# Down's operand 128 bytes lower in SBUF, and 56 instead of 48 products between a norm's sums and the transposes of its factors

## The chip, the cores and the metric

One core of one Trainium2 chip runs the whole program. The metric is device time in microseconds (us) of one execution, from the hardware profiler; lower is better.

## What is computed

A small transformer on one sequence of 256 tokens with 1024 channels, in float32. Two layers, each made of an FFN, a mixer, a second FFN and a per-layer embedding (ple), and behind them one hybrid layer with an FFN of its own and a last norm. Cut to what the change touches:

```python
def rms_norm(x, g):
    return x * rsqrt(mean(x * x, -1) + EPS) * g

def swiglu(h, w_gate, w_up, w_down):          # 1024 -> 2816 -> 1024
    return (silu(h @ w_gate) * (h @ w_up)) @ w_down

for i in range(2):
    x = x + 0.5 * swiglu(rms_norm(x, g[0]), ...)               # FFN i-0
    x = x + (even_mixer if i == 0 else mla_mixer)(rms_norm(x, g[1]), ...)
    x = x + 0.5 * swiglu(rms_norm(x, g[2]), ...)               # FFN i-1
    x = x + ple(rms_norm(x, g[3]), p[i], ...)
x = x + concat(moba, ssd, pool)(rms_norm(x)) @ w_out            # hybrid
x = x + swiglu(rms_norm(x), ...)                                # the last FFN
```

## The kernel before

Activations lie transposed, channels on the 128 partitions and the 256 tokens along a row, as eight tiles `self.x`. TensorE's float32 is replaced by products of numbers rounded to a short mantissa (fp32r): each operand is split into a high part and the rest, and each weight tile of 128x128 takes three products, high by high, rest by high, high by rest. One product is a weight load of 128x128 and a matmul with 256 columns moving; `mm` (line 163) issues them all. The moving operand of the gate and up projections are the rows `hh`/`hl` (`self.hT`, eight pairs of tiles in the pool `cp`); that of the Down projection are pieces of tiles named `big` (list `aT`, pool `sp`), which also serve elsewhere as work space. All weights stream from memory in pieces of 1 MB (`load_piece`), queued on SP; ACT rounds each half to `whi` (line 259) and DVE forms `wlo` (line 260).

`ffn` calls `fm` for gate and up, 44 column blocks in 22 groups of 48 products (two blocks, 8 inner tiles, 3 products), and then for Down, 8 groups of 66 products. A group fills one of four PSUM banks (`acc`), and `evac` empties it: DVE multiplies by the norm's factors (`scaled`, line 429), ACT takes the Silu, DVE the product, and ACT and DVE split the result into `aT`.

The norm's factor is applied after the product, so gate and up start on rows without it. `Stat.begin` issues four tiny matmuls (`aux<-ones,sqa`) that add the squares; DVE computes a reciprocal root from them; `Stat.finish` issues two transposes (line 302, `aux<-ident,ny`) that spread it over the partitions, and ACT copies it to `rb` (line 99), which `evac` needs. Where these stand in TensorE's stream is written out in `fm` by two counts of products, the pair `when`, counted behind the groups that lead (`k_first`):

```python
        def reached(m):
            if stat is not None and stat.rb is None:
                if stat.r is None and count >= when[0]:
                    stat.begin(m)
                elif stat.r is not None and count >= when[1]:
                    stat.finish(m)
```

(lines 339 to 344; called behind every product of a group that does not lead, and once behind the leading ones.) While `stat.rb` is not there, finished groups are held and then evicted together. `behind` tells the framework's scheduler to place an instruction behind a product; it can come out a little later than asked.

The pairs: (0, 48) with two leading groups for FFN 0-0 (line 124); (48, 96) with one leading group for FFN 0-1, FFN 1-1 and the last FFN (line 461); (12, 60) with two for FFN 1-0 and the hybrid's first projection, set at the end of `ple` (line 552). The even mixer, the mla mixer and both ples use the default (0, 48) of line 330.

Tiles are laid out in SBUF in the order in which the program asks for them. `pad` in line 213 is a tile that nothing uses: 48 floats (192 bytes) on each partition at the head of what the pool `sp` lays out behind it. By the program's own allocation `hh` and `hl` lie at byte 448 modulo 512 of a partition, `big` and the mixers' output operands at 64, the weights at 128.

Of the kernel before, what the change touches and what calls it, by code (L numbers as in the profile page):

```python
# [10 lines left out]
FT = mybir.dt.float32  # L11
# [6 lines left out]
P = 128  # L18
# [22 lines left out]
class Columns:  # L41


    def __init__(self):
        self.at = {}
        self.n = 0
        self.parts = []
# [59 lines left out]
class Kern:  # L107
    def __init__(self, nc, tc, a, es, at):
        self.nc, self.tc, self.a, self.at = nc, tc, a, at

        def pool(name, bufs=1, **k):
            return es.enter_context(tc.tile_pool(name=name, bufs=bufs, **k))

        self.wp = pool("wp")
        self.cp = pool("cp")
        self.sp = pool("sp", 2)
        self.ps = pool("ps", 4, space=bass.MemoryType.PSUM)
        self.px = pool("px", 4, space=bass.MemoryType.PSUM)
        self.takes = []
        self.piece, self.off = -1, PIECE  # L120
        self.halves = None
        self.hold = -1
        self.late = None, None
        self.lead, self.when = 2, (0, 48)
        self.constants()


# [41 lines left out]
    def constants(self):  # L169
        nc, a, cp = self.nc, self.a, self.cp  # L170
        self.cols = cp.tile([P, a["cols"].shape[1]], FT, name="cols")
        self.x = []
        self.raw = [self.wp.tile([P, PIECE], FT, name="wraw", bufs=3) for _ in range(2)]

        def load_x(c, n, eng=nc.sync):
            t = cp.tile([P, n * T], FT, name=f"x{c}")
            eng.dma_start(t, a["xT"][:, c * T : (c + n) * T])
            self.x += [t[:, u * T : (u + 1) * T] for u in range(n)]

        def load_w(i, q, n):  # L180
            o = slice(q * 512, (q + n) * 512)
            nc.sync.dma_start(self.raw[i][:, o], a["wts"][i][:, o])


        self.ones = cp.tile([P, 1], FT, name="ones")
        cp.tile([P, 32], FT, name="pad")
        nc.vector.memset(self.ones, 1.0)
        idle = self.tmp(512, "gu", bufs=3)
        nc.vector.memset(idle, 0.0)
        ps = self.aux()  # L190
        for _ in range(5):
            self.mm(ps[:, :T], idle[:, :P], idle[:, :T])
        load_x(0, 1)
        nc.scalar.dma_start(self.cols, a["cols"])
        load_w(0, 0, 1)
        load_x(1, 1, nc.scalar)
        load_w(0, 1, 1)
        load_x(2, 1, nc.scalar)
        load_w(0, 2, 1)
        load_x(3, 1)  # L200
        load_w(0, 3, 1)
        load_x(4, 2)
        load_w(1, 0, 2)
        load_x(6, 2)
        load_w(1, 2, 2)
        self.ident = cp.tile([P, P], FT, name="ident")
        nc.sync.dma_start(self.ident, a["ident"])
        self.hT = [
            (cp.tile([P, T], FR, name=f"hh{c}"), cp.tile([P, T], FR, name=f"hl{c}"))
            for c in range(D)  # L210
        ]

        self.sp.tile([P, 48], FT, name="pad", bufs=1)
        self.eps = cp.tile([P, 1], FT, name="eps")
        nc.vector.memset(self.eps, EPS)
        nc.scalar.activation(self.tiny(1, "nz"), self.ones, AF.Silu)
# [106 lines left out]
    def prep(self, gain):  # L323
        def f(d):
            return self.split(self.hT[d][0], self.hT[d][1], self.x[d], self.col(gain, d))

        return f
# [109 lines left out]
    def ffn(self, gate, up, down, rstd, half, prep, between=None):  # L437
        nc = self.nc
        aT = []

        def evac(i, ps):
            gu = self.tmp(512, "gu", bufs=3)
            self.scaled(gu, ps, rstd.rb)
            sg = self.tmp(T, "sg", bufs=3)
            self.mark = nc.scalar.activation(sg, gu[:, :T], AF.Silu).ins  # L445
            pr = self.tmp(T, "pr", bufs=3)
            nc.vector.tensor_tensor(pr, sg, gu[:, T:], op=OP.mult)  # L447
            f = i // 2
            if f % 2 == 0:
                self.a2 = self.big(FR)  # L450
            o = (f % 2) * 512
            hi, lo = self.a2[:, o : o + T], self.a2[:, o + T : o + 512]
            self.split(hi, lo, pr)
            aT.append((hi, lo))

        chunks = []
        for f in range(F):
            for src, c0 in (gate, up):
                chunks.append((src, (c0 + f * P, P)))
        lead = self.lead or 1  # L460
        self.fm(chunks, self.hT, evac, k_first=lead, stat=rstd, when=(48, 96) if lead == 1 else self.when)
        self.lead = 0
        if between:
            between()

        def evac_d(d, ps):
            if half:
                nc.vector.scalar_tensor_tensor(self.x[d], ps, 0.5, self.x[d], op0=OP.mult, op1=OP.add)  # L468
            else:
                nc.vector.tensor_tensor(self.x[d], ps, self.x[d], op=OP.add)  # L470
            if prep:
                prep(d)
            self.sq_add(self.x[d], d, own=prep is None and d == D - 1)
            if prep is None and d < D - 1:
                self.final(d)

        self.fm([(down, (d * P, P)) for d in range(D)], aT, evac_d, sizes=[1] * D, k_first=True)
# [24 lines left out]
    def ple(self, i, proj, rstd, post, gain, fill=None):  # L502
        nc = self.nc
        ys = [self.big(), self.big()]

        def evac(c, ps):
            n = ps.shape[-1]
            z = self.tmp(512, "gu", bufs=3)[:, :n]
            with self.tc.high_priority():
                self.scaled(z, ps, rstd.rb)  # L510
                nc.scalar.activation(z, z, AF.Sigmoid)
                o = slice((c % 4) * T, (c % 4) * T + n)
                y = ys[c // 4][:, o]
                nc.vector.tensor_tensor(y, z, proj[c // 4][:, o], op=OP.mult)  # L514
                for u in range(n // T):
                    self.sq_add(y[:, u * T : (u + 1) * T], c + u, c >= 6)

        self.fm([(("ple_w_gate", i), (d * P, P)) for d in range(D)], self.hT, evac, [2, 2, 2, 1, 1], k_first=True, stat=rstd)
        self.late = (self.piece + 2, 1), self.mark
        post_r = self.sq_end().now()  # L520
        more = fill() if fill else None


        def col(d):
            return ys[d // 4][:, (d % 4) * T : (d % 4 + 1) * T]

        with self.tc.high_priority():
            m = None
            for d in range(D + 1):
                if d < D:  # L530
                    with self.behind(m):
                        nc.vector.tensor_tensor(col(d), col(d), post_r.pb, op=OP.mult)
                        m = nc.vector.scalar_tensor_tensor(
                            self.x[d], col(d), self.col(post, d), self.x[d], op0=OP.mult, op1=OP.add
                        ).ins
                    g = self.col(gain, d)
                    hi, lo = self.hT[d]
                    nc.scalar.activation(hi, self.x[d], AF.Copy, scale=g)  # L538
                    sq = nc.scalar.activation(col(d), self.x[d], AF.Square).ins
                if d:  # L540
                    hi, lo = self.hT[d - 1]
                    with self.behind(m):
                        m = nc.vector.scalar_tensor_tensor(  # L543
                            lo, self.x[d - 1], self.col(gain, d - 1), hi.bitcast(FT), op0=OP.mult, op1=OP.subtract
                        ).ins
            with self.behind(m):
                nc.vector.tensor_tensor(ys[0], ys[0], ys[1], op=OP.add)
                m = nc.vector.tensor_tensor(ys[0][:, :512], ys[0][:, :512], ys[0][:, 512:], op=OP.add).ins
        self.sq = [ys[0][:, :T], ys[0][:, T : 2 * T]]
        self.marks = (sq, m)  # L550
        self.hold = 3
        self.lead, self.when = 2, (12, 60)
        return more


# [1096 lines left out]
```

## Time and profile before

| | |
|---|---|
| median of 3 runs | 1332.64 us (1331.53 to 1332.75) |
| the profiled execution's own time | 1331.74 us |
| its span in the profile | 1330.0 us |
| TensorE (PE) busy | 1305.2 us, 98% |
| VectorE (DVE) busy | 922.9 us, 69% |
| ScalarE (ACT) busy | 726.4 us, 55% |
| GpSimd (POOL) busy | 76.1 us, 6% |
| granted clock of TensorE, mean over the run | 0.995 |
| memory traffic | 235.5 MB, 177 GB/s |

The span is the time between the first and the last recorded instruction; the execution's own time has some 1.7 us more around it. Matmuls are pipelined: a row of n matmuls in the timeline lasts from the start of the first to the end of the last, and one alone lasts 0.28 us though the next starts 0.11 to 0.12 us behind it. In a row such as `acc<-hh,whi 128*128 128x256 f32 x8` the moving operand stands first, the weights second, and x8 counts the matmuls taken together.

### The profile page before, as it was taken

The page shows a single profiled execution, that of the slowest core. Times are in us where ns is not written, and L with a number is a line of the kernel's source. Part 1 is how long each engine was busy: PE and PEld are TensorE (multiplying, and loading weights), DVE is VectorE, ACT ScalarE, POOL GpSimd, SP SyncE. Part 2 cuts the span into 40 slices and gives each one's busy share as a digit, 9 for nine tenths or more (in the row PEclk, how much of TensorE's full clock was granted, in tenths as well). Part 3 has the DMA queues.
Part 4 walks back from the last instruction along what each step waited for, and adds up shares of the span by engine and source line. Part 5 has one row for each costly group of instructions (what it writes and reads, how often), then busy time and mean ns, then how long its engine had stood idle before and what let it go on. Part 6 is the DMA issues. An engine that isn't in the chain of part 4 may idle for free.

```text
span 1330.0 us, 25894 instructions
## 1 busy us (share of the span) xinstructions
PE 1305.2 (98%) x10830; PEld 1275.3 (96%) x10830; DVE 922.9 (69%) x1528; ACT 726.4 (55%) x1110; POOL 76.1 (6%) x94
## 2 busy tenths in 40 slices
PE   9999999999999999999999899999998999999997
PEld 8999999899999999999999679999998998999997
DVE  7866657978666657966556867777557897867643
ACT  6555546646555456655545566554445685655542
POOL 3000010002000001000000002000002000200001
PEclk9999999999999999999999999999999999999999
DMA  8755555245555554465546313655555344455541
GB/s 320 262 190 187 174 196 181 95 162 188 190 190 188 185 210 159 163 219 190 190 162 220 127 64 116 205 191 196 185 186 183 135 142 143 164 207 198 194 159 64
DMA packets 34933, 235.50 MB, mean 177 GB/s; under 512 B 4016, under 2 KB 4784, under 8 KB 7168
## 3 DMA queue, kind: packets, MB, share of 16 engines
q1 hardware_dynamic: 32976, 229.98, 50.0%
q0 software_dynamic: 832, 2.47, 0.6%
q8 instruction: 85, 1.39, 0.4%
q10 hardware_dynamic: 1008, 1.40, 0.3%
q14 instruction: 32, 0.26, 0.1%
HBM read 232.78 MB, written 1.05 MB: 176 GB/s over the span
## 4 chain that ended last, share of the span: by engine, by line
PE 74%; DVE 5%; ACT 2%; issue 1%; DVEq 0%; ACTq 0%
PE acc L163 69%; PE aux L163 4%; DVE wlo L260 1%; PE aux L302 0%; ACT whi L259 0%; PE aux L1130 0%; DVE big L1175 0%; DVE qs L961 0%; ACT hh L273 0%; ACT at L1132 0%; DVE kv L961 0%; ACT ae L1122 0%; ACT big L949 0%; DVE big L514 0%; DVE big L429 0%
## 5 line engine op out<-in xcount | busy, mean ns | idle before, releaser
L260 DVE TENSOR_TENSOR wlo<-wraw,whi 128x1024 fp32r<-128x1024 f32 (+1 forms) x440 | 531.7, 1222 | 253.1 <-ACT whi L259 164.2
L259 ACT ACTIVATE whi<-wraw 128x1024 fp32r<-128x1024 f32 (+1 forms) x440 | 451.3, 1047 | 308.4 <-PE acc L163 221.4
L163 PE MATMUL acc<-hh,whi 128*128 128x256 f32 x2192 | 328.3, 279 | 3.4 <-ACT hh L538 3.1
L163 PE MATMUL acc<-hl,whi 128*128 128x256 f32 x2192 | 327.3, 278 | 0.2 <-DVE hl L543 0.2
L163 PE MATMUL acc<-hh,wlo 128*128 128x256 f32 x2192 | 326.3, 278 | 1.1 <-DVE wlo L260 1.1
L163 PEld LDWEIGHTS acc<-hh,whi 128*128 128x128 f32 x2192 | 286.0, 188 | 5.4 <-ACT hh L538 3.8
L163 PEld LDWEIGHTS acc<-hh,wlo 128*128 128x128 f32 x2192 | 286.0, 188 | 1.6 <-DVE wlo L260 1.4
L163 PEld LDWEIGHTS acc<-hl,whi 128*128 128x128 f32 x2192 | 286.1, 188 | 0.4 <-DVE hl L543 0.4
L163 PE MATMUL acc<-big,whi 128*128 128x256 f32 x2032 | 271.7, 280 | 0.0
L163 PEld LDWEIGHTS acc<-big,whi 128*128 128x128 f32 x2032 | 256.4, 189 | 0.4 <-ACT big L270 0.2
L163 PE MATMUL acc<-big,wlo 128*128 128x256 f32 x1016 | 161.7, 280 | 0.0
L163 PEld LDWEIGHTS acc<-big,wlo 128*128 128x128 f32 x1016 | 137.6, 189 | 0.0
L318 POOL TENSOR_TENSOR sqa<-sqa,sq 128x256 f32<-128x256 f32 x72 | 65.0, 903 | 1119.2 <-ACT sq L317 1117.1
L429 DVE TENSOR_TENSOR gu<-acc,rb 128x512 f32<-128x512 f32 (+1 forms) x122 | 81.9, 678 | 50.4 <-PE acc L163 50.1
L273 ACT ACTIVATE hh<-x,cols 128x256 fp32r<-128x256 f32 x64 | 30.3, 503 | 82.7 <-DVE x L468 79.2
L270 ACT ACTIVATE big<-pr 128x256 fp32r<-128x256 f32 x114 | 45.9, 409 | 52.0 <-DVE pr L447 50.2
L445 ACT ACTIVATE sg<-gu 128x256 f32<-128x256 f32 x110 | 44.8, 411 | 38.7 <-DVE gu L429 38.5
L271 DVE TENSOR_TENSOR big<-pr,big 128x256 fp32r<-128x256 f32 x114 | 47.8, 426 | 21.0 <-ACT big L270 21.0
L447 DVE TENSOR_TENSOR pr<-sg,gu 128x256 f32<-128x256 f32 x110 | 45.4, 419 | 2.2 <-ACT sg L445 2.2
L274 DVE SCALAR_TENSOR_TENSOR hl<-x,cols,hh 128x256 fp32r<-128x256 f32 x64 | 38.0, 619 | 8.6 <-ACT hh L273 8.3
L163 PE MATMUL aux<-big 128*128 128x128 f32 (+5 forms) x260 | 37.6, 310 | 0.8 <-DVE big L683 0.8
L317 ACT ACTIVATE sq<-x 128x256 f32<-128x256 f32 x62 | 23.9, 405 | 24.3 <-DVE x L470 18.2
(297 smaller groups left out, 788.5 us busy)
## 6 DMA issues: line engine op xcount, KB each, us to landing
wraw<-wts SPq DMA_DIRECT2D x216, 1024.0 KB, 4.9
wraw<-wts SPq DMA_DIRECT2D x4, 256.0 KB, 4.9
wraw<-wts SPq DMA_DIRECT2D x2, 512.0 KB, 5.4
x<-xT SPq DMA_DIRECT2D x2, 256.0 KB, 5.2
big<-wsT POOLq DMA_DIRECT2D x1, 512.0 KB, 13.3
gu<-pT ACTq DMA_DIRECT2D x2, 256.0 KB, 3.1
out<-big SPq DMA_DIRECT2D x2, 256.0 KB, 2.3
out<-big ACTq DMA_DIRECT2D x2, 256.0 KB, 2.5
```

Of the source, the lines that this page charges most:

```text
L163: return self.nc.tensor.matmul(out, l, r, start=start, stop=stop, skip_group_check=True).ins
L259: nc.scalar.activation(hi[:, i], s, AF.Copy)
L260: nc.vector.tensor_tensor(lo[:, i], s, hi[:, i].bitcast(FT), op=OP.subtract)
L270: a = nc.scalar.activation(hi, src, AF.Copy)
L271: b = nc.vector.tensor_tensor(lo, src, hi.bitcast(FT), op=OP.subtract)
L273: a = nc.scalar.activation(hi, src, AF.Copy, scale=scale)
L274: b = nc.vector.scalar_tensor_tensor(lo, src, scale, hi.bitcast(FT), op0=OP.mult, op1=OP.subtract)
L317: nc.scalar.activation(q, src, AF.Square)
L318: self.mark = nc.gpsimd.tensor_tensor(self.sq[0], self.sq[0], q, op=OP.add).ins
L429: self.nc.vector.tensor_tensor(out.rearrange("p (u t) -> p u t", u=n), ps.rearrange("p (u t) -> p u t", u=n), rb.unsqueeze(1).to_broadcast ...
L445: self.mark = nc.scalar.activation(sg, gu[:, :T], AF.Silu).ins
L447: nc.vector.tensor_tensor(pr, sg, gu[:, T:], op=OP.mult)
```

## The change

The unused tile `pad` shrinks from 48 to 16 floats, so that every tile behind it in the pool moves down by 128 bytes: `big` and the mixers' output operands come to lie at byte 448 modulo 512, as `hh` and `hl` do (those do not move). And in the three written pairs the second count rises by eight, so that the transposes are asked for 56 instead of 48 products behind the sums. The default pair of line 330 stays.

```diff
@@ Kern.__init__ (line 124)
-        self.lead, self.when = 2, (0, 48)
+        self.lead, self.when = 2, (0, 56)
@@ Kern.constants (line 213)
-        self.sp.tile([P, 48], FT, name="pad", bufs=1)
+        self.sp.tile([P, 16], FT, name="pad", bufs=1)
@@ Kern.ffn (line 461)
-        self.fm(chunks, self.hT, evac, k_first=lead, stat=rstd, when=(48, 96) if lead == 1 else self.when)
+        self.fm(chunks, self.hT, evac, k_first=lead, stat=rstd, when=(48, 104) if lead == 1 else self.when)
@@ Kern.ple (line 552)
-        self.lead, self.when = 2, (12, 60)
+        self.lead, self.when = 2, (12, 68)
```

## Rows read from the trace of the kernel before

**Rows 1.** The page: busy time by engine, and the chain's share by line.

```profile
PE 1305.2 (98%) x10830; PEld 1275.3 (96%) x10830; DVE 922.9 (69%) x1528; ACT 726.4 (55%) x1110; POOL 76.1 (6%) x94
...
PE acc L163 69%; PE aux L163 4%; DVE wlo L260 1%; PE aux L302 0%; ACT whi L259 0%; PE aux L1130 0%; DVE big L1175 0%; DVE qs L961 0%; ACT hh L273 0%; ACT at L1132 0%; DVE kv L961 0%; ACT ae L1122 0%; ACT big L949 0%; DVE big L514 0%; DVE big L429 0%
```

**Rows 2.** Windows: stretch, length, busy (instructions) PE, PEld, DVE, ACT, POOL; clock, DMA, GB/s.

```profile
40.00:90.00 50.00, 50.00 (x427) 50.00 (x426) 37.67 (x51) 26.17 (x39) 0.00 (x0) 1.00 0.62 212
140.00:190.00 50.00, 50.00 (x427) 50.00 (x426) 27.57 (x32) 22.53 (x31) 4.41 (x6) 1.00 0.50 175
...
440.00:490.00 50.00, 50.00 (x443) 50.00 (x443) 28.12 (x36) 25.24 (x36) 4.40 (x6) 1.00 0.54 190
560.00:610.00 50.00, 50.00 (x444) 50.00 (x443) 36.38 (x50) 26.16 (x38) 0.00 (x0) 1.00 0.63 211
660.00:710.00 50.00, 50.00 (x427) 50.00 (x426) 26.43 (x30) 23.16 (x32) 4.41 (x6) 1.00 0.53 187
850.00:900.00 50.00, 50.00 (x444) 50.00 (x443) 34.75 (x46) 25.60 (x38) 0.00 (x0) 1.00 0.59 197
945.00:995.00 50.00, 50.00 (x427) 50.00 (x426) 26.77 (x31) 22.64 (x31) 4.06 (x6) 1.00 0.52 179
1165.00:1215.00 50.00, 50.00 (x443) 50.00 (x443) 35.29 (x47) 24.96 (x38) 0.00 (x0) 1.00 0.58 202
```

**Rows 3.** Timeline of PE, Down of FFN 1-0 and of FFN 0-1: start, length.

```profile
659.12 5.35 PE L163 MATMUL acc<-big,whi 128*128 128x256 f32 x44
...
705.76 5.35 PE L163 MATMUL acc<-big,whi 128*128 128x256 f32 x44
...
439.72 5.15 PE L163 MATMUL acc<-big,whi 128*128 128x256 f32 x44
...
484.60 5.15 PE L163 MATMUL acc<-big,whi 128*128 128x256 f32 x44
```

**Rows 4.** Timeline of PE, FFN 0-0, from the sums to the transposes.

```profile
19.05 0.50 PE L163 MATMUL aux<-ones,sqa 128*128 128x1 f32 x4
19.41 2.13 PE L163 MATMUL acc<-hh,whi 128*128 128x256 f32 x16
21.38 2.05 PE L163 MATMUL acc<-hl,whi 128*128 128x256 f32 x16
23.27 2.05 PE L163 MATMUL acc<-hh,wlo 128*128 128x256 f32 x16
25.15 0.40 PE L163 MATMUL acc<-hh,whi 128*128 128x256 f32 x2
25.38 0.38 PE L302 MATMUL aux<-ident,ny 128*128 128x128 f32 x2
```

**Rows 5.** Timeline of PE, FFN 0-1, around the transposes.

```profile
323.57 1.10 PE L163 MATMUL acc<-hh,wlo 128*128 128x256 f32 x8
324.58 0.40 PE L302 MATMUL aux<-ident,ny 128*128 128x128 f32 x2
...
325.76 1.10 PE L163 MATMUL acc<-hl,whi 128*128 128x256 f32 x8
```

**Rows 6.** The same in FFN 1-1; six more such at 509.28, 549.12, 725.29, 1011.90, 1051.18, 1154.05.

```profile
833.43 1.10 PE L163 MATMUL acc<-hh,wlo 128*128 128x256 f32 x8
834.38 0.38 PE L302 MATMUL aux<-ident,ny 128*128 128x128 f32 x2
...
835.50 1.07 PE L163 MATMUL acc<-hl,whi 128*128 128x256 f32 x8
```

**Rows 7.** Timelines of ACT, DVE and PE, FFN 1-0, behind the transposes.

```profile
549.54 0.39 ACT L99 ACTIVATE rb<-aux 128x256 f32<-128x256 f32 x1 [0.43 <-PE aux L302]
...
548.09 3.49 DVE L260 TENSOR_TENSOR wlo<-wraw,whi 128x1024 fp32r<-128x1024 f32 x3
551.49 1.88 DVE L429 TENSOR_TENSOR gu<-acc,rb 128x512 f32<-128x512 f32 x3
...
553.42 1.07 PE L163 MATMUL acc<-hh,whi 128*128 128x256 f32 x8
```

## The prediction

> **What bounds the kernel now.** I read the page first. TensorE (PE) is busy for 98% of the span, and in the chain that ended last 69% of the span is the one line that issues all products [rows 1]. A change that adds no product and moves no load can therefore act in two ways: through a wait of PE, or through how fast one product follows another. So the next view is the busy table by windows of 50 us, put inside stretches where PE has no idle time. The granted clock is 1.00 in all of them, DMA share and the load of DVE and ACT differ little, the products are of one shape, and yet some windows hold 427 products and others 443 or 444 [rows 2]. There are two rhythms and nothing between. The timeline gives them exactly: in the Down projection each of the 8 groups of 66 products shows one x44 row, so from the second to the eighth start lie 396 products: 46.64 us in layer 1's first FFN, 44.88 us in layer 0's second [rows 3]. That is 117.78 ns and 113.33 ns per product. Both engines of PE have work throughout, so the 4.44 ns are paid for each product of a slow stretch.
>
> Which stretch has which rhythm, from the windows and the timeline, an FFN being 912 gate/up products behind the transposes (910 in the first) and 528 of Down:
> - FFN 0-0: gate slow, Down slow. FFN 0-1: gate slow, Down fast. FFN 1-0, FFN 1-1 and the last FFN: gate fast, Down slow [rows 2].
>
> A stretch keeps its rhythm for hundreds of products, through changes of weight buffer, of PSUM bank and of DMA load. I find a change at two kinds of places only: where the stream is broken by the sums and transposes of a norm, and where the moving operand goes from the rows (hh, hl) to Down's `big`. The change touches both.
>
> **At the transposes.** The single start stamps of the slow rhythm repeat every three products (three times 117.78 is 353.33 ns, in steps of 118, 118 and 117). Behind the norm's sums the stream was slow at all nine sites, and it began at the same place of that three-step. Then come the two transposes. In seven of seven sites where they came 48 products behind the sums and found their operand ready (0.38 us for the pair), the eight-product rows behind them take 1.07 us, the fast rhythm; the rows ahead of them take 1.10 [rows 6]. In FFN 0-0 the transposes were placed 50 products behind the sums (16+16+16+2), were just as clean at 0.38, and the stream stayed slow [rows 4]. In FFN 0-1 they came after 48, but had to wait: 0.40 us for the pair, a start some 0.07 us late, and the stream stayed slow [rows 5]. So the instant at which the transposes cut the stream decides, and that instant has a period of three products: 48 is 0 modulo 3, 50 is 2, and **56 is 2**. A cut 56 products behind the sums meets the same place of the three-step as the one that left FFN 0-0 slow.
>
> **At the switch to Down.** In the kernel before, the program's allocation puts hh and hl at byte 448 modulo 512, `big` at 64. At this switch the rhythm went from fast to slow three times, from slow to fast once, and stayed slow once. In the start stamps, which the trace keeps finer than the views print them, fast stretches lie on a grid of 6.67 ns that shifts with the moving operand's place, by half a step between 448 and 64. With `big` at 448 there is no shift, and I expect Down to go on in the rhythm of its gate.
>
> **The change part by part**, in products times 4.44 ns:
> - Transposes at 56, gates: FFN 1-0, 1-1 and the last are fast now and turn slow. 900+912+912 = 2724 products, 12.1 us lost. FFN 0-0 and 0-1 stay slow: 0.
> - The hybrid's first projection has the same setting and some 36 fast products behind its transposes: 0.16 us lost.
> - Down: behind a slow gate it is slow. Four of five are slow now: 0. FFN 0-1's fast one, with the 48 products of the ple projection behind it (576), turns slow: 2.56 us lost.
> - FFN 0-1's transposes find their operand ready, being 0.94 us later: 0.08 us won. At the other five sites nothing waited: 0.
> - Later factors: the copy of the row factors on ACT follows the transposes at once, and DVE reads it in the first scaled eviction. In FFN 1-0 that copy ended at 549.93, while DVE was in three weight splits until 551.58; the bank that the eviction frees is taken by PE only at 553.42 [rows 7]. Eight products later (0.94 us) the copy ends at 550.87, still under the splits. At four sites the cut moves from a group's end to 8 products into the next, so that four finished groups instead of three wait for it; in FFN 1-0 that is so already (60, and a group is 48), without idle time of PE. I take 0. Without that cover one more split comes first and the bank is late by at most 1.2 us at a site (3.49/3).
> - The pad moves everything allocated behind it, the out-projections' operands included: three of 192 products go from 64 to 448. No row shows them at 448; if all changed rhythm it would be 576×4.44 = 2.6 us either way. I take 0, since at the switch to Down the rows show both signs, and keep ±2.6.
> - No DMA, no SP or POOL instruction changes its place in its queue, and no load is added.
>
> Sum: 12.1+0.16+2.56−0.08 = **14.7 us lost**. The profiled execution took 1331.74 us (span 1330.0 and 1.7 around it); 1346.5. It lies 0.9 under the median of the runs, 1332.64, so the forecast is 1347.4.
>
> A rule of the skill speaks against all of this. Rows first: with the same shape, clock and neighbours the product took 117.78 and 113.33 ns [rows 3], and the change came at the switch of operand. The Trainium skill, "SBUF — State Buffer", section "Who interferes with whom", says of SBUF's ports that "PE and ACT never wait on anyone". By that rule alone the place of an operand costs nothing; the rows show a loss of 4%, though not that a port is its cause. It is the rival "nothing matters" below.
>
> **The rivals.**
> - **All fast** (the other side). 56 gives a clean, fast cut everywhere, and all Downs follow their gates. For it: 56 leaves DVE 0.94 us more, which cures FFN 0-1's late cut [rows 5]; with only one clean cut at 50, the class modulo 3 rests on one site [rows 4], and its slowness may come from something else, as its place in the first FFN among small pieces of weight. Against it: that cut was clean at 0.38. It wins 910 and 912 products in FFN 0-0 and 0-1 (4.04+4.05), four Downs of 528 (9.38), and 0.08: 17.6 us, so about 1315; the leading groups behind Downs may add 1.5. It decides as soon as a cut at 56 does what one at 48 does with operands ready.
> - **56 as 48, site by site.** FFN 0-0 and 0-1 stay slow, the three fast gates stay fast and their Downs turn fast (1584 products, 7.04 us won), FFN 0-1's Down turns slow (2.56 lost): 4.5 won, 1328.2.
> - **A mixture.** The scheduler put FFN 0-0's transposes two products late [rows 4]; it may do so elsewhere, so that sites fall into different classes. Each gate that is fast, with its Down, is worth 1440×4.44 = 6.4 us: one such site gives 1341, two give 1335.
> - **Down's place does not decide.** Gates turn slow as forecast, the Downs stay as they are: 1344.9. This lies in the forecast's own range.
> - **Nothing matters.** Neither place nor cut is the cause, only something that the change leaves alone: 1332.6.
>
> **How the numbers follow.** Forecast 0.60; its own range is 1344.5 to 1350 (the out-projections' ±2.6, the eviction's 1.2). All fast 0.16, 56 as 48 0.07, mixture 0.14, nothing 0.03. The range from 1326 to 1350 holds all but the all-fast case, 0.84. A measurement of this kernel can tell about 0.2% (2.7 us) from no change. Faster by more than that: all fast, 56 as 48, and mixtures with three fast sites (0.06), 0.29. Within it: nothing, and mixtures with two (0.02), 0.05. Slower: the forecast and mixtures with one (0.06), 0.66.
>
> **What would show it.** The windows of the changed kernel: 427 products in 50 us at every gate and Down if the forecast holds, 443 or 444 in all of them if all is fast. At the cut: the transposes' row at 0.38, then eight-product rows of 1.10 (slow) or 1.07 (fast). In Down: x44 rows of 5.35 or 5.15 us. If the gates are slow and Downs differ from their gates, the step on the switch is wrong; if gates are fast behind a clean cut at 56, the class modulo 3 is wrong, and with it the sign. Idle time of PE ahead of the first products after the cut would show the eviction wrongly costed.

## The result, and the profile after

The changed kernel took 1342.73 us (median of 4 runs, 1341.86 to 1348.93) against 1332.70 us before: a ratio of 1.0089, 95% interval 1.0062 to 1.0116. It is slower, by some 10 us. The forecast was 1347.4 us, range 1326 to 1350, slower at 0.66. The profiled execution took 1342.79 us, 11.05 more than that of before (span 1341.1).

How often one and the same program differs from one execution to the next matters for what follows, so the changed kernel was timed once more among the experiments: 12 runs, 1335.85 to 1342.86, median 1337.88, ratio 1.0036 (1.0019 to 1.0053). The kernel before, beside it, took 1328.95 to 1339.07 in 17 runs, median 1334.47. So the changed kernel is slower both times, by 10.0 us and by 3.4 us, but its time is no single number; the last experiment and the table of all profiles show why.

The windows of 50 us of the changed kernel, with the columns of [rows 2]; FFN 0-1's gate (330) is added, and each row is named below by its first microsecond:

```profile
40.00:90.00 50.00, 50.00 (x443) 50.00 (x442) 38.85 (x52) 27.17 (x40) 0.00 (x0) 1.00 0.66 221
140.00:190.00 50.00, 50.00 (x444) 50.00 (x443) 28.77 (x33) 24.07 (x33) 4.41 (x6) 1.00 0.51 179
440.00:490.00 50.00, 50.00 (x427) 50.00 (x426) 28.82 (x34) 23.01 (x32) 4.79 (x7) 1.00 0.52 179
330.00:380.00 50.00, 50.00 (x427) 50.00 (x426) 32.95 (x45) 25.10 (x36) 0.00 (x0) 1.00 0.56 190
560.00:610.00 50.00, 50.00 (x427) 50.00 (x426) 34.20 (x46) 24.70 (x37) 0.00 (x0) 1.00 0.60 206
660.00:710.00 50.00, 50.00 (x427) 50.00 (x426) 27.62 (x32) 22.64 (x31) 4.43 (x6) 1.00 0.50 173
850.00:900.00 50.00, 50.00 (x427) 50.00 (x426) 33.59 (x44) 24.13 (x36) 0.00 (x0) 1.00 0.56 190
945.00:995.00 50.00, 50.00 (x427) 50.00 (x426) 27.73 (x33) 23.10 (x32) 3.75 (x5) 1.00 0.53 186
1165.00:1215.00 50.00, 50.00 (x427) 50.00 (x426) 35.10 (x50) 26.25 (x41) 0.00 (x0) 1.00 0.53 180
```

Read the count of PE: 427 is slow (117.78 ns a product), 443 or 444 fast (113.33). The three gates that were fast are slow (560, 850, 1165). So is FFN 0-1's Down (440), which was fast. Every Down has the rhythm of its gate. One thing was not forecast: FFN 0-0 (40, 140) is fast, gate and Down. By "cut" the text means the point where a norm's two transposes interrupt the stream of products; a cut is clean where they waited for nothing (0.38 us for the pair), and fast or slow by the stream behind it.

PE's timeline around the transposes, in FFN 0-0 (26.20) and FFN 1-1 (837.33), answers to [rows 4, 6]:

```profile
25.26 1.10 PE L163 MATMUL acc<-hh,whi 128*128 128x256 f32 x8
26.20 0.38 PE L302 MATMUL aux<-ident,ny 128*128 128x128 f32 x2
26.33 1.16 PE L163 MATMUL acc<-hl,whi 128*128 128x256 f32 x8
...
836.39 1.10 PE L163 MATMUL acc<-hh,whi 128*128 128x256 f32 x8
837.33 0.38 PE L302 MATMUL aux<-ident,ny 128*128 128x128 f32 x2
837.47 1.19 PE L163 MATMUL acc<-hl,whi 128*128 128x256 f32 x8
```

Both cuts are clean (0.38) and stand 56 products behind their sums, yet one leaves the stream fast (the row behind it 1.16, its first product taking longer) and the other slow (1.19). In FFN 0-1 the pair of transposes now takes 0.38 too, where it had waited [rows 5].

One more difference lies outside the forecast. Behind the first ple PE waits 1.6 us for the rows, in both kernels, and then the changed kernel's clock is granted at half, 1.2 instead of 2.4 GHz. First the changed kernel's window, then that of the same stretch in the kernel before:

```profile
527.40:530.60 3.20, 3.20 (x17) 3.20 (x17) 3.10 (x8) 2.02 (x6) 0.00 (x0) 0.50 0.00 0
```

```profile
531.20:534.40 3.20, 3.20 (x29) 3.20 (x29) 3.10 (x8) 2.07 (x6) 0.00 (x0) 1.00 0.00 0
```

17 products instead of 29 in 3.2 us: 12 products, 1.4 us. It does not belong to the change: in the second profile of the changed kernel the clock was granted in full behind the same wait of 1.6 us.

The account, in us (products times 4.44 ns where a rhythm changed; at the three gates the eight products just ahead of the cut count too, which stood behind it before and were fast):

| place | forecast | measured |
|---|---|---|
| gates of FFN 1-0, 1-1, last | +12.1 | +12.1 (900+912+912) |
| FFN 0-1's Down with the ple projection | +2.56 | +2.56 (576) |
| FFN 0-1's transposes | -0.08 | -0.09 |
| FFN 0-0, gate and Down | 0 | -6.4 (904+528) |
| first projections of ple, mla, ple (cut at 48, not edited) | 0 | +1.0 (94+47+94) |
| out-projections | 0, ±2.6 | +0.5 (45+72) |
| half clock behind the first ple | none | +1.4 |
| hybrid's first projection; rows behind FFN 0-0's Down and in the even mixer | +0.16 | -0.4 |
| sum | +14.7 | +10.7, of 11.05 |

Two lines contradict the class modulo 3 as the prediction had it. FFN 0-0 is fast at 56. And ple and mla, which the edit of the counts does not touch and which were cut clean at 48 in both kernels, were fast before [rows 6] and are slow now. Something else than the count has changed what the cut finds. The pad moves not only `big`: by the program's allocation the squares `sqa` and `sq`, the stationary operands of the sums, went from 320 to 192 modulo 512. Counted modulo 256 bytes, 320 is half a step (128 bytes) from the rows' 448, and 192 is the rows' own place.

### The profile page after: what moved, and what is told of

It is laid out like the page before. It is cut to its first block, busy times and chain, and to the rows that moved or that the text cites. A ratio compares the mean times of both kernels' runs of the same rounds, so it can differ in the third digit from the quotient of the medians.

```text
span 1341.1 us, 25901 instructions
## 1 busy us (share of the span) xinstructions
PE 1316.7 (98%) x10830; PEld 1286.7 (96%) x10830; DVE 922.4 (69%) x1528; ACT 726.6 (54%) x1110; POOL 76.2 (6%) x94
## 4 chain that ended last, share of the span: by engine, by line
PE 75%; DVE 4%; ACT 2%; issue 1%; DVEq 0%; ACTq 0%
PE acc L163 71%; PE aux L163 4%; DVE wlo L260 1%; PE aux L302 0%; PE aux L1130 0%; DVE big L1175 0%; ACT whi L259 0%; DVE qs L961 0%; DVE kv L961 0%; DVE big L514 0%; ACT ae L1122 0%; ACT big L949 0%; ACT big L1179 0%; ACT at L1132 0%; DVE big L1497 0%
## 5 line engine op out<-in xcount | busy, mean ns | idle before, releaser
L163 PE MATMUL acc<-hh,wlo 128*128 128x256 f32 x2192 | 330.4, 280 | 0.9 <-DVE wlo L260 0.9
L163 PE MATMUL acc<-hl,whi 128*128 128x256 f32 x2192 | 330.8, 280 | 0.2 <-DVE hl L543 0.2
L163 PEld LDWEIGHTS acc<-hh,whi 128*128 128x128 f32 x2192 | 289.3, 188 | 5.1 <-ACT hh L538 3.8
L163 PEld LDWEIGHTS acc<-hh,wlo 128*128 128x128 f32 x2192 | 289.3, 188 | 1.5 <-DVE wlo L260 1.3
L163 PEld LDWEIGHTS acc<-hl,whi 128*128 128x128 f32 x2192 | 289.2, 188 | 0.4 <-DVE hl L543 0.4
```

Source lines behind the costliest of these rows:

```text
L163: return self.nc.tensor.matmul(out, l, r, start=start, stop=stop, skip_group_check=True).ins
```

## The experiments

**Theory 1.** Three steps. The sums leave the stream at a place of its three-step; where that is hangs on the address of the sums' stationary operand. The transposes, so many products later, cut it there, and one place in three gives the fast rhythm. Down goes on in its gate's rhythm if its moving operand lies where the rows do. **Rival A**: the count alone decides. **Rival B**: `big`'s place decides, for gates too.

The two places can be set apart with the program's instructions unaltered: `nb`, a scratch of 128 bytes, lies between `sqa` and `big`, so its number of buffers moves `big` and leaves `sqa` where it is. All that is laid out behind `nb` moves with `big`, among it `ny`, the weights of the transposes; that `ny`'s place decides is a third rival, **C**. Most of the kernels below ran once, so their times are single numbers; what is read from them is the rhythm of each gate and Down in the profiled execution.

### The pad alone

```diff
-        self.sp.tile([P, 48], FT, name="pad", bufs=1)
+        self.sp.tile([P, 16], FT, name="pad", bufs=1)
```

> The pad of 16 floats alone; the counts stay at 48, so the instructions of every engine are those of before and only addresses differ (sqa and sq from 320 to 192, big and the outputs of the mixers from 64 to 448 modulo 512). Theory 1 (the sums leave the slow stream at a place of its three-step that hangs on where sqa lies, and the transposes then find another place): the gates of FFN 1-0, 1-1 and the last lose their rhythm of before, the first projections of ple and mla are slow as in the changed kernel, FFN 0-0 (cut at 50, the same class as 56) is fast with its Down; 1336 to 1343 us. Rival (the count modulo 3 alone decides, as predicted): the three gates stay fast, their Downs follow them, FFN 0-1's Down turns slow; about 1328 us.

1336.41 us. The same instructions in the same order as before, other addresses. Windows, in FFN 1-0 (560, 660) and FFN 1-1 (850, 945):

```profile
560.00:610.00 50.00, 50.00 (x444) 50.00 (x443) 37.39 (x53) 28.18 (x41) 0.00 (x0) 1.00 0.62 211
660.00:710.00 50.00, 50.00 (x443) 50.00 (x443) 27.87 (x33) 23.70 (x32) 4.01 (x6) 1.00 0.53 184
850.00:900.00 50.00, 50.00 (x427) 50.00 (x426) 34.00 (x45) 23.74 (x36) 0.00 (x0) 1.00 0.54 188
945.00:995.00 50.00, 50.00 (x427) 50.00 (x426) 27.34 (x32) 23.49 (x32) 3.76 (x5) 1.00 0.54 189
```

FFN 1-1's gate, cut clean at 48 as before, turned slow: rival A is out. But FFN 1-0 and the last stayed fast, both ples and mla stayed fast too, against theory 1's forecast for them, and FFN 0-0 was slow at 50. With `sqa` at 192 the sums do not leave the stream at one place, as the table of all profiles shows.

### The counts alone

The three pairs of the change, the pad left at 48.

> The counts of 56 alone, all addresses as before. Theory 1 and the prediction agree here: with sqa where it was, 56 is the class of FFN 0-0's slow cut at 50, all five gates are slow (427 products in 50 us), about 12 us lost in three of them, Downs as before: 1343 to 1346 us. Rival (the count does nothing, the place of sqa and big made the gates slow): the three gates stay fast, about 1332 us.

1343.98 us. The gates, in FFN 1-0, 1-1 and the last:

```profile
560.00:610.00 50.00, 50.00 (x427) 50.00 (x427) 34.17 (x47) 25.39 (x36) 0.00 (x0) 1.00 0.60 209
850.00:900.00 50.00, 50.00 (x427) 50.00 (x426) 33.22 (x45) 24.54 (x36) 0.00 (x0) 1.00 0.56 191
1175.00:1225.00 50.00, 50.00 (x426) 50.00 (x426) 33.22 (x45) 24.72 (x36) 0.00 (x0) 1.00 0.57 195
```

All slow, with every address as before: 56 instead of 48 costs the three gates by itself. The Downs were not all as before: FFN 0-1's, which had been fast behind a slow gate, was slow.

```profile
440.00:490.00 50.00, 50.00 (x427) 50.00 (x426) 27.22 (x31) 23.66 (x32) 4.41 (x6) 1.00 0.49 173
```

FFN 0-0's gate was fast at 56, and its Down slow. Its timeline shows how it stands apart:

```profile
19.26 0.61 PE L163 MATMUL aux<-ones,sqa 128*128 128x1 f32 x4 [0.65 <-POOL sqa L318]
```

The squares of the first norm arrive with the first loads, and in this execution the sums waited 0.65 us for them. They then leave the stream at another place than sums that follow a product at once (the table of all profiles).

### Down's operand alone

```diff
-            b = self.tiny(n, "nb", I32)
+            b = self.tiny(n, "nb", I32, bufs=1)
```

> Down's operand alone: the pad stays at 48, and the scratch nb gets one buffer instead of two, so that big and the mixers' outputs lie at 448 while sqa and sq stay at 320; counts 48, the instructions of every engine as before. Theory 1: gates as before (1-0, 1-1 and the last fast, 0-0 and 0-1 slow), and each Down in the rhythm of its gate: three Downs won (7.0 us), FFN 0-1's lost (2.6): about 1328 us. Rival (the place of big, not that of sqa, changes what the sums find): the gates change as in the run with the pad of 16 and 48 products, 1336 to 1343 us.

1322.39 us, faster than before, again with the same instructions. Gate and Down of FFN 0-0 (40), 0-1 (340, 440), 1-0 (560, 650), and Down of 1-1 (930):

```profile
40.00:90.00 50.00, 50.00 (x444) 50.00 (x443) 39.46 (x52) 27.78 (x40) 1.23 (x1) 1.00 0.65 222
340.00:390.00 50.00, 50.00 (x427) 50.00 (x426) 32.55 (x46) 25.55 (x36) 0.00 (x0) 1.00 0.54 186
440.00:490.00 50.00, 50.00 (x427) 50.00 (x426) 28.82 (x33) 22.30 (x31) 4.41 (x6) 1.00 0.50 173
560.00:610.00 50.00, 50.00 (x444) 50.00 (x443) 34.66 (x48) 26.52 (x37) 0.00 (x0) 1.00 0.63 213
650.00:700.00 50.00, 50.00 (x444) 50.00 (x443) 26.71 (x32) 24.36 (x32) 3.71 (x5) 1.00 0.54 190
930.00:980.00 50.00, 50.00 (x444) 50.00 (x443) 29.84 (x36) 23.91 (x33) 3.77 (x5) 1.00 0.55 192
```

Each Down has its gate's rhythm, and the three gates kept theirs: as expected, and rival B is out. So is rival C: `ny` moved here and no gate changed by it, and in the run with the sums' operand alone (below) `ny` stays and gates change. The 6 us below the forecast are FFN 0-0, whose sums waited in this execution and whose gate and Down were fast (1438 products, 6.4 us).

### Down's operand, and 57 products

The same, with the pairs (0, 57), (48, 105), (12, 69).

> As the run with Down's operand alone, and the transposes 57 products behind the sums, a multiple of three, at the six sites. Theory 1: with sqa at 320 a cut at 57 does what one at 48 does, but FFN 0-1's comes late enough to find its operand; all five gates fast and all five Downs behind them: 4.0+4.05+9.4 us won, about 1315 us. Rival (only the distance in products, not its class, decides, 48 being fast by chance): 57 is slow as 56 was, 1343 to 1346 us.

1315.90 us (4 runs, 1315.31 to 1322.43), ratio 0.9888 (0.9855 to 0.9920). All five gates and Downs are fast. Gates of FFN 0-0 and 0-1, Down of 0-1:

```profile
40.00:90.00 50.00, 50.00 (x444) 50.00 (x443) 38.56 (x52) 27.20 (x39) 0.00 (x0) 1.00 0.65 221
...
330.00:380.00 50.00, 50.00 (x444) 50.00 (x442) 34.51 (x47) 26.00 (x38) 0.00 (x0) 1.00 0.57 193
440.00:490.00 50.00, 50.00 (x444) 50.00 (x443) 29.49 (x32) 26.43 (x37) 4.45 (x6) 1.00 0.55 196
```

One product more than in the changed kernel and `sqa` left in place: 27 us. A fixed distance of 48 is not what makes a cut fast.

### The sums' operand alone

Pad 16 and `nb` with three buffers: `sqa` at 192, `big` at 64, counts 48.

> The complement of the run with Down's operand alone: pad 16 and nb with three buffers, so that sqa and sq lie at 192 as in the changed kernel, while big and the mixers' outputs stay at 64; counts 48, the instructions as before. Theory 1 (the place of sqa sets what the sums leave behind): at least one of the three gates that were fast turns slow, as in the run with the pad of 16 and 48 products, and the Downs go on as they please: 1335 to 1342 us. Rival (sqa's place does nothing): gates and Downs as before, about 1332 us.

1336.90 us. Gates of FFN 1-0, 1-1, last:

```profile
560.00:610.00 50.00, 50.00 (x443) 50.00 (x443) 34.66 (x48) 26.04 (x38) 0.00 (x0) 1.00 0.62 212
850.00:900.00 50.00, 50.00 (x427) 50.00 (x426) 34.25 (x45) 23.75 (x36) 0.00 (x0) 1.00 0.54 187
1165.00:1215.00 50.00, 50.00 (x426) 50.00 (x426) 33.35 (x45) 24.63 (x36) 0.00 (x0) 1.00 0.56 190
```

Moving the squares alone made two of three gates slow. The one that stayed fast, FFN 1-0, is the one whose sums do not read `sqa`: behind a ple the squares lie in `big` tiles, which stayed at 64.

### Down's operand at 192 and at 320

57 products, `nb` with three or four buffers; four scratch tiles behind `big` are halved for room.

> As the run with 57 products and big at 448, but with big at 192 modulo 512 (nb with three buffers; four small scratch tiles behind big are halved to make room). Theory 1 with a grid of 256 bytes (8 cycles of 32 bytes): 192 and 448 are one place, each Down goes on in the rhythm of its fast gate, 1315 to 1317 us. Rival (the rows' very place modulo 512 is needed): fast gates, Downs slow as in the kernel before, about 12 us more, 1328 us.

> The same with big at 320 modulo 512 (nb with four buffers). Theory 1 with a grid of 256 bytes: 320 is the place 64 of the kernel before, five fast gates and five slow Downs (2688 products with the ple projection, 11.9 us), about 1328 us. Rival (Down's place does nothing once its gate is fast): 1315 to 1317 us.

1323.94 and 1330.92 us. Down of FFN 0-1 and 1-1 with `big` at 192, then gate of FFN 1-1 and Down of 0-1 and 1-1 with it at 320:

```profile
440.00:490.00 50.00, 50.00 (x444) 50.00 (x443) 29.49 (x32) 26.42 (x37) 4.60 (x7) 1.00 0.56 200
930.00:980.00 50.00, 50.00 (x444) 50.00 (x443) 29.66 (x36) 24.37 (x35) 3.08 (x5) 1.00 0.55 191
```

```profile
850.00:900.00 50.00, 50.00 (x444) 50.00 (x443) 35.30 (x47) 24.86 (x37) 0.00 (x0) 1.00 0.55 190
...
440.00:490.00 50.00, 50.00 (x427) 50.00 (x426) 27.48 (x31) 23.41 (x31) 4.42 (x6) 1.00 0.49 172
940.00:990.00 50.00, 50.00 (x427) 50.00 (x426) 26.39 (x32) 23.19 (x31) 3.75 (x5) 1.00 0.52 184
```

192 acts as 448, 320 as 64: at the four places tried, they count modulo 256 bytes. The eight cycles in the expectation are an estimate (the grid of 6.67 ns is eight periods of 1.2 GHz); no run shows what is read in one. The times are off by one FFN each: at 192 FFN 1-0 was slow, gate and Down (its sums read `big`, which had left the place 64), at 320 FFN 0-0's gate, whose sums waited.

### The first sums 12 products later

```diff
-        self.lead, self.when = 2, (0, 57)
+        self.lead, self.when = 2, (12, 69)
```

> As the run with 57 products and big at 448, but in FFN 0-0 the sums come 12 products later (12, 69). There the first squares arrive with the loads, and in some executions the sums waited for them about 1 us, in others not, so that they left the stream at another place; FFN 0-0's gate and Down are then 6.3 us slower or faster from one execution to the next. Theory: 12 products (1.4 us) later they never wait, the cut at 57 is fast in each execution, and the times lie at 1314 to 1317 us with none near 1322. Rival (the spread has another cause): some executions stay near 1322 us.

A miss: 1331.04, 1315.28, 1318.84, 1316.74, 1323.50 us. In the profiled execution, the slowest, FFN 0-0's sums did not wait and the cut was fast; then this came:

```profile
30.08 1.07 PE L163 MATMUL acc<-hh,wlo 128*128 128x256 f32 x8
31.59 1.18 PE L163 MATMUL acc<-hh,whi 128*128 128x256 f32 x8 [0.44 <-DVE gu L429]
```

The factors came 12 products later, so the evictions did, and PE waited 0.44 us for a bank. Behind that wait the stream was slow for the remaining 863 products and for Down:

```profile
40.00:90.00 50.00, 50.00 (x427) 50.00 (x426) 38.35 (x51) 27.15 (x39) 0.00 (x0) 1.00 0.65 229
```

The eviction, which the prediction had costed at nothing for 8 products, was not free in this execution, with the transposes 19 products later than in the kernel before (69 against 50). FFN 1-0 was slow too, its sums reading `big`.

### The rows moved instead

```diff
-        cp.tile([P, 32], FT, name="pad")
+        cp.tile([P, 64], FT, name="pad")
```

with the pad of 16 and 57 products.

> 57 products, and the 128 bytes taken out of the pad ahead of sqa are put in ahead of the rows instead: hh, hl and ident move from 448 to 64, sqa stays at 320, big at 64 as before, so rows and Down's operand are again at one place, but now the sums' operands (320 and 64) are at that place too modulo 256. If the sums' own address decides (absolute): all gates and Downs fast as with 57 and big at 448, 1315 to 1317 us, or 1322 where FFN 0-0 is slow. If their place against the rows' decides (relative): as with sqa at 192 and the rows at 448, some gates with their Downs slow, 1322 to 1342 us.

1340.10 us. Gates of FFN 0-0, 0-1, 1-1:

```profile
40.00:90.00 50.00, 50.00 (x444) 50.00 (x442) 39.25 (x53) 27.53 (x40) 0.02 (x1) 1.00 0.67 225
340.00:390.00 50.00, 50.00 (x427) 50.00 (x426) 33.02 (x45) 25.01 (x36) 0.00 (x0) 1.00 0.54 184
850.00:900.00 50.00, 50.00 (x427) 50.00 (x427) 33.40 (x45) 24.62 (x36) 0.00 (x0) 1.00 0.54 182
```

Four of five gates slow, their Downs with them, though `sqa` lies at 320 and the count is 57, as in the run of 1315.9 us. The fast one is FFN 0-0's, whose sums waited. So the sums' own address does not decide. What the two runs differ in is the place of the rows against everything else, the sums' operand among it: the reading that the sums' place against the rows' counts fits, but this run alone does not show it. It is also a case of its own: at five of its nine norms the stream left the sums already fast, ahead of any cut, which no other profile shows.

### All sums half a step away

57 products, `big` at 448, and

```diff
-                m = nc.vector.tensor_tensor(ys[0][:, :512], ys[0][:, :512], ys[0][:, 512:], op=OP.add).ins
-        self.sq = [ys[0][:, :T], ys[0][:, T : 2 * T]]
+                self.sq = [self.tmp(T, "sqa") for _ in range(2)]
+                for u, q in enumerate(self.sq):
+                    a, b = u * T, 512 + u * T
+                    m = nc.vector.tensor_tensor(q, ys[0][:, a : a + T], ys[0][:, b : b + T], op=OP.add).ins
```

in `ple`, and (12, 63) for FFN 0-0.

> 57 products and big at 448, sqa at 320, with two more edits. The sums behind a ple (FFN 1-0 and the hybrid) read their squares from two sqa tiles instead of big, so that all sums' operands lie half a grid step from the rows. And in FFN 0-0 the pair is (12, 63): the sums 12 products later, so that they need not wait for the first squares, and 51 products, a multiple of three, so that the evictions are not late as they were with (12, 69). Theory: all five gates and Downs are fast in each execution, 1313 to 1317 us, none over 1319. Rival (a gate's rhythm is chance, whatever the sums' place): the times spread over 1315 to 1331 us as in the run with the late sums.

1316.42 us (4 runs, 1315.35 to 1317.37), ratio 0.9866 (0.9839 to 0.9894): as expected. Gates of FFN 0-0 and 1-0, the two that the edits were for:

```profile
40.00:90.00 50.00, 50.00 (x444) 50.00 (x443) 39.35 (x53) 27.97 (x41) 0.00 (x0) 1.00 0.66 223
...
560.00:610.00 50.00, 50.00 (x443) 50.00 (x443) 34.51 (x47) 25.94 (x38) 0.00 (x0) 1.00 0.56 190
```

It is the version to keep; its median is not told apart from that of the run with 57 alone, but none of its four runs strays.

### 58 products at three sites

57 products and `big` at 448, and (48, 106) in `ffn`.

> 57 products and big at 448 as before, but 58 in FFN 0-1, FFN 1-1 and the last FFN: the class of three that no run has shown. If one third of the three-step alone gives the fast rhythm, these three gates and their Downs are slow: about 4340 products times 4.44 ns, 19 us more, 1334 to 1336 us (6 more for each of FFN 0-0 and 1-0 that is slow by its own sums). If the class 1 is fast too: 1315 to 1322 us.

1342.52 us. FFN 0-0 (57) and the gates of 0-1 and 1-1 (58):

```profile
40.00:90.00 50.00, 50.00 (x444) 50.00 (x443) 39.23 (x53) 27.37 (x40) 0.00 (x0) 1.00 0.66 220
340.00:390.00 50.00, 50.00 (x427) 50.00 (x426) 32.62 (x44) 25.64 (x36) 0.00 (x0) 1.00 0.54 183
850.00:900.00 50.00, 50.00 (x426) 50.00 (x426) 33.93 (x45) 23.81 (x36) 0.00 (x0) 1.00 0.54 188
```

The gates with 58 are slow, the last FFN's too, and FFN 1-0 by its own sums: 19 and 6 us, as the expectation allowed.

### The changed kernel again

> The changed kernel once more, unaltered, for its spread. If FFN 0-0, whose sums meet the first loads, is fast in some executions and slow in others, the times lie in two groups, near 1342 and 6 to 7 us above, near 1349, and the profiled execution belongs to the first if its windows at 40 and 140 us hold 443 or 444 products, to the second if they hold 427. If the spread is of another kind, no such groups.

Groups there are, but not those expected: eight runs lie from 1335.85 to 1338.40 and four from 1341.06 to 1342.86. In the profiled one (1342.86) FFN 0-0 was slow, against the expected link, and the last FFN fast:

```profile
40.00:90.00 50.00, 50.00 (x427) 50.00 (x426) 37.24 (x50) 26.33 (x39) 0.00 (x0) 1.00 0.62 211
140.00:190.00 50.00, 50.00 (x427) 50.00 (x426) 27.48 (x32) 22.53 (x31) 4.44 (x6) 1.00 0.51 176
1175.00:1225.00 50.00, 50.00 (x444) 50.00 (x443) 35.51 (x48) 25.38 (x37) 0.00 (x0) 1.00 0.58 193
1275.00:1325.00 50.00, 50.00 (x444) 50.00 (x443) 23.16 (x26) 23.67 (x32) 5.00 (x6) 1.00 0.40 142
```

So it is not FFN 0-0 alone: between the two profiles of this kernel FFN 0-0 and the last FFN changed rhythm, each worth some 6.4 us with its Down. Both profiled executions had four slow FFNs and took 1342.8 us; three and five would give 1336.4 and 1349.2 us, and the 16 runs do lie near 1337, 1342 and 1349. That is an estimate from the two, since the executions that were not profiled show no gate.

### All fourteen profiles together

Every cut where neither sums nor transposes waited, of the FFNs, the ples, mla and the hybrid, by the sums' operand against the rows modulo 256 and by the count modulo 3; the figures are cuts that left the stream fast, of all:

| | count 0 | count 1 | count 2 |
|---|---|---|---|
| half a step away (128 bytes) | 59 of 59 | 0 of 3 | 0 of 6 |
| at the same place | 17 of 36 | not tried | 2 of 13 |

The second row looks like chance, but the start stamps, which the trace keeps to the nanosecond (the views round them to 10), show an order in it. Behind the sums the slow rhythm begins at one of two places of its three-step, one product apart. They can be told by the gap between the third and the fourth product behind the sums: 115 to 118 ns at the first place, which is that of the kernel before, 120 ns at the second. Half a step away all 68 cuts stand at the first; at the same place 24 stand at the first and 17 at the second (without the run with the rows moved, a case of its own: 8 cuts, four of them fast already ahead of the cut). In the four cases where the sums waited this gap says nothing, but the stamps of all products up to the cut, taken by threes against an even beat, put each at the second place. With these four, in thirteen profiles, cuts that left the stream fast, of all:

| | count 0 | count 1 | count 2 |
|---|---|---|---|
| sums left at the first place | 72 of 72 | 0 of 3 | 0 of 17 |
| at the second place | 0 of 16 | not tried | 5 of 5 |

So in these thirteen profiles the class modulo 3 has no exception where the transposes waited for nothing; it is counted from where the sums leave, and that is what the sums' address, or a wait of theirs, changes. The two lines that contradicted it in the changed kernel are of this kind: FFN 0-0 (56 products), both ples and mla (48) left from the second place, the other sites (56) from the first. This order was read out of the traces afterwards, and no run was made to test it; nor does the record show what picks one of the two places at the rows' own address.

And Down behind its gate: at the rows' place it kept the gate's rhythm in 50 of 50. Half a step away 10 of 10 fast gates had a slow Down, and of 10 slow gates two had a fast one.

## Why the prediction was right, and where not

**What bounds the kernel** held. The rhythm of the products and a clock step account for 10.7 of the 11.05 us; PE's busy time rose by 11.5 us (1316.7 against 1305.2 in [rows 1]), and no load or eviction joined the path.

**56 is 2 modulo 3, so the gates are slow** was right in its result and right as a law for the kernel before: the counts alone did it (12 us in three gates), and the table has no exception where the sums' operand lies half a step away. In the changed kernel itself it was not the whole reason. The step that failed is the assumption under it, that the sums leave the stream at a fixed place. That held at nine of nine sites before because `sqa` happened to lie half a step from the rows. The pad took it to the rows' place, and in the changed kernel's profile four of nine norms left from the second place: FFN 0-0's cut at 56 was fast by it, and the ples' and mla's at 48 were slow. The prediction listed `big` and the out-projections among what the pad moves, not the sums' operands. That the class rested on one clean site, at 50, it had said itself.

**FFN 0-0 stays slow, 0** was therefore wrong in the profiled execution: 6.4 us less. The measured 1342.73 lies in the wide range, but outside the forecast's own (1344.5 to 1350); it is the mixture with one fast site, 1341 us at the price it gave, with 1.4 us of half clock and 1.0 of the ples and mla on top, neither of them in the sum. The mixture's own reason did not occur: the scheduler put all six pairs at 56. How far the time moved is in part luck: the same kernel's median was 1337.88 in the second timing.

**A measurement can tell 0.2%** was too sure. It rested on three runs within 1.2 us; in 17 runs the kernel before spread over 10 us.

**Down follows its gate** was right without exception. FFN 0-1's Down cost the 2.56 us of the forecast, and FFN 0-0's was fast behind a fast gate. The rival that Down's place does not decide is out.

**The evictions at nothing** was right for eight products: in the changed kernel's profile PE waited for no eviction (DVE line 429). The run with the first sums 12 products later showed a wait of 0.44 us there, and a rhythm lost.

**All fast**, the rival on the other side, fell in the three gates that it needed. What it describes exists, at 1316 us, with a count of 57 and the sums' operand left alone.

**Nothing matters**, that a place costs nothing, is out: the run with Down's operand alone, the same instructions with tiles moved, took 1322.4 us instead of 1332.9, 6.4 us of it in FFN 0-0, whose sums waited, and the rest, some 4 us, in the Downs. The Trainium skill, "SBUF — State Buffer", section "Who interferes with whom", which the prediction weighed for this rival, says of SBUF's ports that PE waits on no other engine; no run here shows whether a port is behind the price of a place, so the runs neither bear that sentence out nor refute it.

Still open: why a product takes 113.33 or 117.78 ns, and what picks the place at which the sums leave the stream when their weights lie at the rows' place. The trace shows starts, not their reasons. Places other than 64, 192, 320 and 448 were not tried, nor were the weights moved.

## What to carry to other kernels

Where TensorE is the bound, count products in windows of equal length before looking for waits: a stream without idle time can have two speeds, and what sets the speed may be a handful of small matmuls ahead of it and the addresses of their operands. Before moving a tile by resizing one ahead of it, list every tile that moves with it and which engine reads each; here the intended move of Down's operand was worth 4.5 us (three Downs won, one lost), and in the profile of the pad alone the squares that moved with it cost 6.4 us (FFN 1-1). And when a program's addresses, not its instructions, decide, time it several times and profile it more than once: one execution of the changed kernel shows a fast gate where another shows a slow one.

## What was not expected of the hardware

- The address of a stationary operand (`sqa`, four matmuls of 0.50 us together) decided 4 us in the 900 products behind it: with it half a step of 256 bytes from the rows 59 of 59 cuts at a multiple of three were fast, at the rows' place 17 of 36. In thirteen of the fourteen profiles the stream left the sums at one of two places, one product apart, and that place with the count modulo three told every cut whose transposes waited for nothing.
- A wait of 0.44 us in a fast stretch left it slow for 863 products: 3.8 us, nine times the wait itself.
- The clock was granted at 0.50 for 3.2 us behind a wait of 1.6 us in one profile of the changed kernel, and at 1.00 behind the same wait in another profile of it and in the kernel before.
